# The decoder step's feed-forward: an up projection of seven products instead of eight, a down projection of its own, and the sample tokens' indexer on TensorE

## The chip, the cores and the metric

The kernel runs on one core of one Trainium2 chip. The metric is the device time of one execution in microseconds (us), the median of several runs.

## The reference, cut to what matters

One layer of a decoder handles 2048 prompt tokens and 8 sample tokens. All arrays are float32, with D = 1024 and D_FF = 2816.

```python
z = rmsnorm(x) @ w_in                       # one input projection, columns split between the mixers
# A: an indexer scores all earlier keys, the best 256 of each query are attended (8 heads of 64)
score = sum_h w[t,h] * relu(q_idx[t,h] . k_idx[s]) ;  idx = top_k(score, 256)
# B: pooling over trailing windows;  C: attention to 256 memory tokens
x = x + concat(A, B, C) @ w_out
u = rmsnorm(x) @ w_up                       # 1024 -> 2 * 2816, [g, v]
g, v = conv3(u)                             # causal, per channel
x = x + (silu(g) * v) @ w_down              # 2816 -> 1024
```

For the sample tokens the indexer scores 8192 cached keys of each token, which lie in pages: `dots[key, h] = relu(q_idx[h] . k_idx[key])`, weighted and summed over 8 heads.

## The kernel before, in words

Products of float32 are made on TensorE (PE) from two float32r parts, high and low, as three passes: high x high, high x low, low x high. A helper, `split_psum` (L224 ScalarE, L225 VectorE), makes the two parts of a tile: ScalarE (ACT) writes the high part, VectorE (DVE) subtracts it and writes the low one.

The stages follow one another: a first projection with the indexer's scores of the 16 blocks of 128 prompt tokens (0 to about 330 us; matmuls `pj` are the projection, `isc` the scores, which ACT evicts as `rl`); a second projection and the choice of keys (to about 640); attention by four groups of heads over 16 blocks (to 1184; the probabilities are transposed in `apt`, summed with the values in `ax`, and a block's result leaves as `ao` to the DRAM scratch `mix_d`); the output projection (to 1374), which adds the residual and makes the second norm `h`; the feed-forward (to the end).

The feed-forward goes by three chunks of tokens (768, 776 and 504 + 8 sample tokens), and in each over f = 0 to 21 tiles of 128 hidden channels. For each f, two weight tiles `wr` of 512 KB (gate and value) are loaded and split to `uh`, `ul`; 8 k-steps times three passes (L1675 to L1677) go into PSUM `upg` and `upv`; the convolution reads PSUM (ACT L1679, DVE L1680 and L1682); then silu, the product on GpSimd (POOL, L1692) and a split to `ah`, `al`. Every second f the down products `py` (L1717 to L1719) of all blocks are made and DVE adds them to `yacc` in SBUF (L1720).

The sample tokens' mixers are traced behind the output projection. The scheduler puts their instructions, which have a lower priority, into the feed-forward. Their indexer multiplies on POOL (`ipr`, L1244) and sums on DVE (`dots`, L1246).

All ordinary DMAs are issued by the queue of SyncE (SP), in order: one that waits for its data holds those behind it. Indirect DMAs are issued by POOL. The scheduler fixes each engine's order at build time.

Of the kernel before, what the change touches and what calls it, by code (L numbers as in the profile page):

```python
# [9 lines left out]
F32 = mybir.dt.float32  # L10
# [10 lines left out]
EPS = 1e-6  # L21
# [23 lines left out]
PA, PL = 0, 600  # L45
# [5 lines left out]
# the blocks of each group of heads after which a part of the attention to the memory is traced  # L51
# [25 lines left out]
def bias_onehot():  # L77
    """One-hot bucket of T5 distance x - 127 (none below 0)."""
# [9 lines left out]
def tile_decoder(ctx, tc, I, O, C):  # L88
# [27 lines left out]
    # the sum of two halves of 64  # L116
# [3 lines left out]
    # per-partition signs and masks of the stack (hi, lo, hi, lo) x 32  # L120
# [8 lines left out]
    with tc.tile_pool(name="vps", bufs=1, side="right", space=PSUM) as vps, tc.tile_pool(name="vsb", bufs=1) as vsb:  # L129
        # what the first weights wait for comes first  # L130
# [49 lines left out]
    h_d = dram.tile([KC, 128, S + NS], F32, name="h_d")  # L180
    snew_d = dram.tile([NS, 1], F32, name="snew_d")
# [9 lines left out]
    def rsqrt(ss, p, n, scale):  # L191
        """1 / sqrt(ss * scale + EPS) on [p, n]"""
# [13 lines left out]
    def rsqrt_g(ss, p, n, scale):  # L206
        """the same on GpSimd"""
# [14 lines left out]
    def split_psum(ps, hi, lo):  # L222
        """hi (float32r) and lo (float32r) of a float32 tile"""
# [7 lines left out]
    def split_g(raw, hi, lo, g):  # L231
        """the same, with GpSimd for ScalarE"""
# [7 lines left out]
    def parts_of(b, xh, xl):  # L240
        """what project takes"""
# [4 lines left out]
    def load_x_T(b, xpool, xps, sq):  # L246
        """Block b's tokens, channel-major, in two float32r parts; b = NB: the sample tokens."""
# [17 lines left out]
        # for the second projection  # L265
# [7 lines left out]
    def project(p, xh, xl, outs, spare=None):  # L273
        """outs: (psum, hi weights, lo weights) of [KC] chunks"""
# [25 lines left out]
    # the queries' gains, with the scale of the logits, along the free dimension  # L300
# [1471 lines left out]
```

## Time and profile before

| | |
|---|---|
| runs | 2963.34, 2968.76, 2970.40 us; median 2968.76 |
| profiled execution, its span | 2975.3 us |
| PE busy | 2787.9 us, 94% |
| DVE, ACT, POOL busy | 2241.5, 1365.5, 1187.9 us |
| first and last feed-forward matmul | 1373.8 and 2960.7 us |

The span is the profiled execution's own time; it is 6.5 us above the median of the runs. A busy PE in the profile counts overlapping matmuls once; the pace of matmuls is read from the distance between their starts, since the duration of one covers its pipeline too.

### The profile page before, as it was taken

The numbers are of one execution on the slowest core, as the hardware profiler recorded it, in microseconds if no ns is written. First come the engines' busy times: TensorE is split into PE (matmuls) and PEld (weight loads), VectorE is DVE, ScalarE is ACT, GpSimd is POOL, SyncE is SP. The second block draws the span as 40 slices with busy tenths as digits, with TensorE's granted clock in tenths as the row PEclk, the third lists the DMA queues.
The fourth block names the chain that finished last, engine by engine and source line by source line (L and its number), as shares of the span: only waits on it lengthen the run. The fifth ranks groups of instructions, "written<-read, shape, count | busy, mean of one in ns | idle before, by whom it ended". The sixth has DMA issues, their size and how long they took to land.

```text
span 2975.3 us, 41646 instructions
## 1 busy us (share of the span) xinstructions
PE 2787.9 (94%) x14707; PEld 2428.2 (82%) x14707; DVE 2241.5 (75%) x4459; ACT 1365.5 (46%) x2307; POOL 1187.9 (40%) x1097
## 2 busy tenths in 40 slices
PE   8988788869999999999999999999989999999997
PEld 7877456658988988888988888989878889878886
DVE  5788987967888888446899989898787665666554
ACT  5667686457777777345222222232223333233332
POOL 2333434835745564002888998310436100000000
PEclk9999899879999999999999999999999999999999
DMA  5321334372213223653222222233343322243331
GB/s 183 124 91 54 124 101 123 102 215 80 82 55 99 62 83 99 190 149 115 71 74 75 86 64 73 69 122 121 96 129 92 109 80 82 82 153 106 93 92 53
DMA packets 310311, 301.68 MB, mean 101 GB/s; under 512 B 27444, under 2 KB 272245, under 8 KB 309317
## 3 DMA queue, kind: packets, MB, share of 16 engines
q1 hardware_dynamic: 305236, 285.28, 31.2%
q0 software_dynamic: 4864, 13.73, 1.6%
q8 instruction: 116, 1.90, 0.3%
q14 instruction: 95, 0.77, 0.1%
HBM read 236.36 MB, written 62.89 MB: 101 GB/s over the span
## 4 chain that ended last, share of the span: by engine, by line
PE 58%; DVE 12%; POOL 6%; DMA 3%; issue 2%; ACT 1%; SPq 0%; DVEq 0%; ACTq 0%; POOLq 0%
POOL ipr L1244 4%; PE py L1717 4%; PE upv L1677 4%; PE upv L1675 4%; PE py L1719 4%; PE upv L1676 4%; PE py L1718 4%; PE upg L1677 4%; PE upg L1675 4%; PE upg L1676 4%; PE apt L1055 3%; PE as L1038 2%; DVE dots L1246 2%; PE ax L1058 2%; PE ax L1059 2%
## 5 line engine op out<-in xcount | busy, mean ns | idle before, releaser
L1244 POOL TENSOR_TENSOR ipr<-G,qbc 128x512 f32<-128x512 f32 x256 | 371.1, 1479 | 66.4 <-DVE dots L1246 55.4
L1032 POOL TENSOR_TENSOR t<-R,first 128x128 f32<-128x128 f32 (+15 forms) x128 | 289.0, 2290 | 209.4 <-PE apt L1055 178.9
L1692 POOL TENSOR_TENSOR ct<-ct,ct 128x768 f32<-128x768 f32 (+2 forms) x65 | 118.6, 1824 | 623.8 <-DVE ct L1686 305.6
L1720 DVE TENSOR_TENSOR yacc<-yacc,py 128x512 f32<-128x512 f32 (+1 forms) x408 | 273.1, 680 | 117.8 <-PE py L1719 95.6
L1717 PE MATMUL py<-dh,ah 128*128 128x512 f32 (+1 forms) x704 | 279.8, 399 | 16.0 <-DVE yacc L1720 10.7
L1719 PE MATMUL py<-dh,al 128*128 128x512 f32 (+1 forms) x704 | 275.3, 397 | 3.9 <-DVE al L1697 3.9
L1718 PE MATMUL py<-dl,ah 128*128 128x512 f32 (+1 forms) x704 | 278.1, 395 | 0.0
L224 ACT ACTIVATE uh<-wr 128x1024 fp32r<-128x1024 f32 x132 | 139.6, 1058 | 292.9 <-PE upv L1676 97.3
L1676 PE MATMUL upg<-fhl,uh 128*128 128x390 f32 (+3 forms) x748 | 258.0, 345 | 5.0 <-issue 3.0
L225 DVE TENSOR_TENSOR ul<-wr,uh 128x1024 fp32r<-128x1024 f32 x132 | 176.7, 1339 | 110.4 <-ACT uh L224 110.2
L1676 PE MATMUL upv<-fhl,uh 128*128 128x390 f32 (+3 forms) x748 | 256.9, 343 | 0.0
L1675 PE MATMUL upg<-fhh,uh 128*128 128x390 f32 (+2 forms) x704 | 241.0, 342 | 5.2 <-DVE ct L1682 3.5
L1675 PE MATMUL upv<-fhh,uh 128*128 128x390 f32 (+2 forms) x704 | 240.1, 341 | 3.5 <-ACT ct L1679 2.0
L1677 PE MATMUL upg<-fhh,ul 128*128 128x390 f32 (+2 forms) x704 | 240.7, 342 | 2.8 <-issue 2.8
L1677 PE MATMUL upv<-fhh,ul 128*128 128x390 f32 (+2 forms) x704 | 239.4, 340 | 0.0
L225 DVE TENSOR_TENSOR pl<-apt,ph 128x512 fp32r<-128x512 f32 (+1 forms) x320 | 204.2, 658 | 24.2 <-ACT ph L224 21.9
L1040 DVE CUSTOM_DVE_ANT_0 t<-as,t 128x512 f32<-128x512 f32 (+11 forms) x320 | 189.8, 606 | 41.9 <-PE as L1039 36.7
L224 ACT ACTIVATE ph<-apt 128x512 fp32r<-128x512 f32 (+1 forms) x320 | 173.1, 581 | 62.0 <-PE apt L1055 32.5
L1246 DVE TENSOR_REDUCE dots<-ipr 128x16 f32<-128x512 f32 x256 | 171.8, 679 | 27.5 <-POOL ipr L1244 27.2
L1717 PEld LDWEIGHTS py<-dh,ah 128*128 128x128 f32 (+1 forms) x704 | 132.7, 189 | 44.5 <-DVE yacc L1720 16.5
L1055 PE MATMUL apt<-ident,t 128*128 128x128 f32 x1088 | 164.9, 274 | 3.4 <-DVE pl L225 1.9
L353 ACT ACTIVATE rl<-isc 128x768 f32<-128x768 f32 (+9 forms) x176 | 138.0, 822 | 59.7 <-PE isc L350 42.9
(578 smaller groups left out, 7676.1 us busy)
## 6 DMA issues: line engine op xcount, KB each, us to landing
wr<-in_w_up_dram SPq DMA_DIRECT2D x132, 512.0 KB
dr<-in_w_down_dram SPq DMA_DIRECT2D x66, 512.0 KB
xt<-in_x_prompt_dram SPq DMA_DIRECT2D x16, 512.0 KB
xh_d<-xh SPq DMA_DIRECT2D x16, 512.0 KB
xl_d<-xl SPq DMA_DIRECT2D x16, 512.0 KB
xh<-xh_d SPq DMA_DIRECT2D x16, 512.0 KB
xl<-xl_d SPq DMA_DIRECT2D x16, 512.0 KB
qa<-qh_d SPq DMA_DIRECT2D x64, 128.0 KB
```

What stands on the lines that cost most here:

```text
L224: nc.scalar.activation(hi, ps, AF.Copy)
L225: nc.vector.tensor_tensor(lo, ps, hi.bitcast(F32), op=OP.subtract)
L1032: nc.gpsimd.tensor_tensor(t[:, :N], backward(R[j][:, :N]), nsel[b], op=OP.add)
L1055: nc.tensor.transpose(pt[:, c, j * 128:j * 128 + 128], pn[j][:, (k + c) * 128:(k + c) * 128 + 128], ident)
L1244: nc.gpsimd.tensor_tensor(pr, G[:, u * 512:u * 512 + 512].rearrange("p (k d) -> p k d", d=32), qbc[:, c, None, 32 * h:32 * h + 32].to_broa ...
L1675: nc.tensor.matmul(d, uh[:, k], hh(k, a, e), start=(k == 0), stop=False)
L1676: nc.tensor.matmul(d, uh[:, k], hl(k, a, e), start=False, stop=False)
L1677: nc.tensor.matmul(d, ul[:, k], hh(k, a, e), start=False, stop=(k == KC - 1))
L1717: nc.tensor.matmul(py[:p], ah[:, r0:r0 + p], dh[:, cs], start=(i == 0), stop=False)
L1718: nc.tensor.matmul(py[:p], ah[:, r0:r0 + p], dl[:, cs], start=False, stop=False)
L1719: nc.tensor.matmul(py[:p], al[:, r0:r0 + p], dh[:, cs], start=False, stop=e)
L1720: nc.vector.tensor_tensor(y[:w, cs], y[:w, cs], py[:w], op=OP.add)
```

## The change

**The up projection.** The tokens go by three pairs of halves, of 344, 344 and 340 tokens (`chunks`). With the two halves of the tokens and the two halves of the 1024 channels, and the gate and value tile of an f, the product is one of 2 x 2 blocks, and it is made by seven products instead of eight (Winograd's form of Strassen's scheme). Seven sums of token halves (`b11`, `t1`, `t2`, `b21`, `t3`, `b22`, `t4`, by `operands`) stay in SBUF as two parts each, and seven weight tiles of 512 channels by 128 are loaded and split per f. Three of the seven come from `w_up` as it is, four from weight sums s1 to s4 that lie in DRAM.

**The weight sums.** They are made in DRAM during attention, by 24 steps that `weight_sums` yields, one after every second block of the last three groups of heads. A step issues plain copies from DRAM to DRAM on SP or accumulating DMAs (`accum_op=add`) on POOL, 16 of each in all and 1.44 MB each. An accumulating one is held back by two tiny DMAs on SP (`gates`), one that reads the block's result `ao` and one that reads the sum that it adds to.

**The down projection.** It no longer adds in SBUF. An f's activation is stored to `act_d`; after an up stage `down` reads it back and sums all 22 f in PSUM, for 5, 5 and 6 blocks by two column halves of 512. The order is up, down, operands, down. `x1_d` is added at the end.

**The sample tokens' indexer** (`sample_scores`) runs in the first projection: its 16 units, two per block from block 2 to 9, each gather 128 x 1024 of keys, transpose them by 8 transposes (`tp<-ident,G`), multiply by 8 matmuls of 64 columns (`tp<-qd,gt`), and evict through ACT (two copies, two relu); POOL multiplies by the head weights, DVE sums. The first projection takes the sample tokens first. The other sample mixers stay in the feed-forward, with a lower priority than before (5500 instead of 1500).

**The output projection** stores `x1_d` and `h_d` for all blocks, in the order 4, 5, 2, 3, 0, 1, 6, 7, 14, 15, 12, 13, 10, 11, 8, 9; the first operands are made after eight of them.

```diff
+        for ops in (((s1, v0, 0), (s3, g0, 0)), ((s1, v1, 1), (s3, v0, 1)), ((s2, s1, 0),), ((s2, g0, 1),),
+                    ((s4, s2, 0),), ((s4, g1, 1),)):
+            for k in range(4):
+                def step(after):
+                    for dst, src, add in ops:
+                        if add:
...
+                            dma(o, after[0:1, 0:1])
+                            dma(o, dst[k, 0:1, 0:1])
+                            nc.gpsimd.dma_start(cut(dst, k), cut(src, k), accum_op=OP.add, max_dma_last_dim=5632)
+                        else:
...
+                            dma(dst[k, 0:1, 0:1], after[0:1, 0:1])
+                            dma(cut(dst, k), cut(src, k))
+                yield step
...
                 dma(mix_d[g, :, q0:q0 + TQ], o)
+                step = next(sums, None) if g and b % 2 else None
+                if step:
+                    step(o)
...
+                product(pa, two_parts(g0), "b11", True)
+                nc.scalar.activation(x1, pa[:, :N], AF.Copy, scale=-1.0)
+                product(pc, two_parts(total(1)), "t1", True)
+                nc.scalar.activation(x5, pc[:, :N], AF.Copy)
+                product(pa, two_parts(total(2)), "t2", False)
+                nc.scalar.activation(u2, pa[:, :N], AF.Copy, scale=-1.0)
+                product(pb, two_parts(g1_), "b21", True)
+                nc.vector.tensor_tensor(u[:, 0, lo], pb[:, :N], x1, op=OP.add)
+                product(pa, two_parts(total(3)), "t3", False)
+                nc.vector.tensor_tensor(u[:, 1, hi], pa[:, :N], x5, op=OP.subtract)
+                product(pc, two_parts(total(4)), "b22", False)
+                nc.vector.tensor_tensor(u[:, 0, hi], pc[:, :N], u2, op=OP.add)
...
+                        "t4", False)
+                nc.scalar.activation(u[:, 1, lo], pa[:, :N], AF.Copy)
...
+                for i in range(nb):
+                    b = slice(i * 128, i * 128 + 128)
+                    nc.tensor.matmul(ys[i], ah[:, b], dh, start=s, stop=False)
+                    nc.tensor.matmul(ys[i], ah[:, b], dl, start=False, stop=False)
+                    nc.tensor.matmul(ys[i], al[:, b], dh, start=False, stop=e)
...
-                            nc.vector.tensor_tensor(y[:w, cs], y[:w, cs], py[:w], op=OP.add)
...
-                        nc.gpsimd.tensor_tensor(pr, G[:, u * 512:u * 512 + 512].rearrange("p (k d) -> p k d", d=32),
-                                                qbc[:, c, None, 32 * h:32 * h + 32].to_broadcast([128, 16, 32]), op=OP.mult)
-                        V.tensor_reduce(dots[:, 16 * u:16 * u + 16, h], pr, axis=AX.X, op=OP.add)
...
+                for j in range(8):
+                    nc.tensor.matmul(pd[:, j], gt[j // 4][:, j % 4, :], qd[:, 2 * c:2 * c + 2].rearrange("p b k h -> p (b k h)"),
+                                     start=True, stop=True)
```

What the change moves stands here at three places. First SP's queue where the output projection ends: before, the feed-forward's first weights (`wr<-in_w_up`) stand among the last blocks' loads (`mt`, `ld`).

```order
L1656 DMA wr<-in_w_up_dram 128x8x128 x2
L1138 DMA ld<-in_x_prompt_dram 128x1024
L1133 DMA mt<-mix_d 128x8x128
L1138 DMA ld<-in_x_prompt_dram 128x1024
L1133 DMA mt<-mix_d 128x8x128
L1138 DMA ld<-in_x_prompt_dram 128x1024
L1656 DMA wr<-in_w_up_dram 128x8x128
L1663 DMA dr<-in_w_down_dram 128x1024
L1656 DMA wr<-in_w_up_dram 128x8x128 x2
L1162 DMA x_d<-yacc 128x1024
```

Now the first weights, `wg<-in_w_up`, stand behind the store of the last block's norm, `h_d<-h`.

```order
L1316 DMA h_d<-h 128x8x128
L1305 DMA x_d<-x_17284 128x1024
L1316 DMA h_d<-h 128x8x128
L1799 DMA dr<-in_w_down_dram 128x512 x3
L1316 DMA h_d<-h 128x8x128
L1799 DMA dr<-in_w_down_dram 128x512 x2
L1715 DMA wg<-in_w_up_dram 128x8x128
L1720 DMA wr<-sum_7671 128x4x128
```

The weights moved from ahead of the last blocks' loads to behind the last block's whole norm.

Second SP's queue in attention, in the last group of heads but one or two: before, results (`mix_d<-ao`) and the next queries (`qa`, `qb`, of two parts and two halves).

```order
L1066 DMA mix_d<-ao 128x128
L1007 DMA mix_d<-ao 128x256
L1066 DMA mix_d<-ao 128x128
L958 DMA qa<-qh_d 64x2x256 x2
L958 DMA qb<-ql_d 64x2x256 x2
L958 DMA qa<-qh_d 64x2x256 x2
L958 DMA qb<-ql_d 64x2x256 x2
L1066 DMA mix_d<-ao 128x128 x3
```

Now a step's gate (1x1) and a copy of a piece of a weight sum (`sum_7674<-sum_7672`, s4 from s2) stand between them.

```order
L1188 DMA mix_d<-ao 128x128 x2
L1055 DMA sum_7674<-ao 1x1
L1056 DMA sum_7674<-sum_7672 32x11264
L1128 DMA mix_d<-ao 128x256
L1079 DMA qa<-qh_d 64x2x256 x2
L1079 DMA qb<-ql_d 64x2x256 x2
L1079 DMA qa<-qh_d 64x2x256 x2
L1079 DMA qb<-ql_d 64x2x256 x2
L1188 DMA mix_d<-ao 128x128
```

The queries' loads come behind the gate and the copy.

Third PE in the first projection, where block 3 is scored: before, score matmuls `isc` alternate with the next block's transposes (`tp<-ident,xt`) and projection (`pj`).

```order
L350 MATMUL isc<-ikst,iqst 128x512
L289 MATMUL pj<-wAh,xl 128x404
L263 MATMUL tp<-ident,xt 128x128 x4
L350 MATMUL isc<-ikst,iqst 128x512
L263 MATMUL tp<-ident,xt 128x128 x4
L350 MATMUL isc<-ikst,iqst 128x512
L286 MATMUL pj<-wAh,xh 128x404
L287 MATMUL pj<-wAl,xh 128x404
L286 MATMUL pj<-wAh,xh 128x404
L287 MATMUL pj<-wAl,xh 128x404
L350 MATMUL isc<-ikst,iqst 128x512
```

Now the same scores alternate with the sample tokens' transposes and matmuls, and the next block's projection stands behind all of them.

```order
L348 MATMUL isc<-ikst,iqst 128x512 x2
L427 MATMUL tp<-ident,G 128x128 x4
L348 MATMUL isc<-ikst,iqst 128x512
L427 MATMUL tp<-ident,G 128x128 x4
L348 MATMUL isc<-ikst,iqst 128x512
L434 MATMUL tp<-qd,gt 128x64 x4
L348 MATMUL isc<-ikst,iqst 128x512
L434 MATMUL tp<-qd,gt 128x64 x4
L427 MATMUL tp<-ident,G 128x128 x4
L348 MATMUL isc<-ikst,iqst 128x512 x2
L427 MATMUL tp<-ident,G 128x128 x4
L434 MATMUL tp<-qd,gt 128x64 x4
```

So for blocks 2 to 8 PE meets the projection only after the scores; from block 9 on the order is as before.

## Rows read from the trace of the kernel before

**Rows 1.** The page: its first line and the busy time of the engines
```profile
span 2975.3 us, 41646 instructions
...
PE 2787.9 (94%) x14707; PEld 2428.2 (82%) x14707; DVE 2241.5 (75%) x4459; ACT 1365.5 (46%) x2307; POOL 1187.9 (40%) x1097
```

**Rows 2.** The table of windows: busy us and count by engine, clock, DMA share, GB/s
```profile
core 0: us, PE busy (x) PEld busy (x) DVE busy (x) ACT busy (x) POOL busy (x), PEclk, DMA share, GB/s
0.00:330.00 330.00, 285.68 (x1454) 243.47 (x1455) 257.23 (x556) 221.19 (x379) 122.26 (x157) 0.94 0.35 119
...
640.00:1184.00 544.00, 508.38 (x3699) 469.51 (x3699) 443.49 (x1330) 411.56 (x890) 299.07 (x138) 0.96 0.29 87
...
1474.00:1874.00 400.00, 380.61 (x1947) 348.07 (x1946) 366.47 (x444) 102.72 (x118) 348.29 (x238) 1.00 0.25 75
2180.00:2570.00 390.00, 390.00 (x2008) 349.88 (x2007) 264.11 (x409) 120.77 (x139) 94.58 (x106) 1.00 0.32 95
```

**Rows 3.** Groups by shape, PE, 1373 us to the end
```profile
L1677 PE MATMUL upg<-fhh,ul 128*128 128x390 f32 x352 | 121.5, 345 | 2.8 <-issue 2.8
...
L1675 PE MATMUL upg<-fxh,uh 128*128 128x512 f32 x176 | 69.6, 395 | 0.0
...
L1675 PE MATMUL upg<-fhh,uh 128*128 128x386 f32 x176 | 60.1, 342 | 3.5 <-DVE ct L1682 3.5
```

**Rows 4.** Timeline of PE at 2000 us (start us, us, instruction)
```profile
2000.06 0.34 PE L1677 MATMUL upg<-fhh,ul 128*128 128x390 f32 x1
...
2002.21 0.34 PE L1677 MATMUL upg<-fhh,ul 128*128 128x390 f32 x1
2002.39 0.40 PE L1717 MATMUL py<-dh,ah 128*128 128x512 f32 x1
...
2002.85 0.39 PE L1719 MATMUL py<-dh,al 128*128 128x512 f32 x1
```

**Rows 5.** Timeline of PE at 855 us
```profile
854.66 0.28 PE L1058 MATMUL ax<-ph,vst 128*128 128x256 f32 x1
...
855.01 0.28 PE L1059 MATMUL ax<-pl,vst 128*128 128x256 f32 x1
```

**Rows 6.** The page's costliest groups: count | busy us, mean ns | idle before
```profile
L1244 POOL TENSOR_TENSOR ipr<-G,qbc 128x512 f32<-128x512 f32 x256 | 371.1, 1479 | 66.4 <-DVE dots L1246 55.4
...
L1720 DVE TENSOR_TENSOR yacc<-yacc,py 128x512 f32<-128x512 f32 (+1 forms) x408 | 273.1, 680 | 117.8 <-PE py L1719 95.6
...
L225 DVE TENSOR_TENSOR pl<-apt,ph 128x512 fp32r<-128x512 f32 (+1 forms) x320 | 204.2, 658 | 24.2 <-ACT ph L224 21.9
...
L224 ACT ACTIVATE ph<-apt 128x512 fp32r<-128x512 f32 (+1 forms) x320 | 173.1, 581 | 62.0 <-PE apt L1055 32.5
L1246 DVE TENSOR_REDUCE dots<-ipr 128x16 f32<-128x512 f32 x256 | 171.8, 679 | 27.5 <-POOL ipr L1244 27.2
```

**Rows 7.** Groups of lines, VectorE and then ScalarE, 1373 us to the end
```profile
L1682 DVE SCALAR_TENSOR_TENSOR ct<-upv,convc,ct 128x768 f32<-128x768 f32 (+2 forms) x66 | 60.9, 922 | 0.5
...
L1679 ACT ACTIVATE ct<-upv,convc 128x768 f32<-128x768 f32 (+2 forms) x66 | 59.9, 907 | 8.3 <-PE upv L1677 8.3
```

**Rows 8.** The chain in order of time, from 917 and from 1470 us
```profile
917.09 7.18 DMA mix_d<-ao
...
1469.99 3.67 DMA dr<-in_w_down_dram
```

**Rows 9.** The table of windows, the first 50 us
```profile
0.00:50.00 50.00, 41.54 (x214) 37.44 (x215) 26.94 (x152) 25.68 (x48) 10.39 (x24) 1.00 0.71 231
```

**Rows 10.** Timeline at the end of the output projection, VectorE, then ScalarE
```profile
1373.99 1.22 DVE L1152 TENSOR_TENSOR yacc<-opy,ld 128x1024 f32<-128x1024 f32 x1
...
1375.31 1.06 ACT L1088 ACTIVATE hn<-yacc 128x1024 f32<-128x1024 f32 x1 [0.83 <-DVE yacc L1152]
...
1380.49 1.15 ACT L1090 ACTIVATE hn<-yacc,rsy 128x1024 f32<-128x1024 f32 x1 [0.29 <-DVE rsy L203]
...
1387.19 1.14 ACT L1172 ACTIVATE hn<-oph,vcol 128x128 f32<-128x128 f32 x4 [3.76 <-PE oph L1095]
```

More of the change, by code (lines that the diff above doesn't have):

```diff
@@ L326, in tile_decoder @@
     junkD = tp_.tile([128, S], mybir.dt.uint8, name="junkD")
-    scp = pool("scp", side="right", stack=scst)
-    for b in range(11, LATE):
-        sc[b] = scp.tile([128, (b + 1) * TQ], F32, name=f"sc{b}")
     dst_ = ExitStack()
@@ L420, in load @@
             return p, xh, xl
-        ahead = load(0)
+        ahead = load(NB)
         wAh = ap_.tile([128, KC, NA], F32R, name="wAh")
@@ L458, in tile_decoder @@
                 dma(v_s.rearrange("l b t h d -> (l b t) (h d)"), z[:p, 552:808])
-                break
+                units = sample_scores(z, pool("six", bufs=2, side="right", stack=sst), ap2, aps)
+                next(units)
+                continue
             q0 = b * TQ
@@ L519, in tile_decoder @@
                 late[b] = iqst, iws
+            if b < 10:
+                for _ in range(2):
+                    with later(SA):
+                        next(units)
+        mapped()
     scl = pool("scl", side="right", stack=scst)
@@ L1015, in tile_decoder @@
             mem_attend(*next(units))
+        sums = weight_sums()
         for g in range(4):
@@ L1127, in tile_decoder @@
             split_psum(raw, woh[k], wol[k])
-        n0 = bounds[1] // TQ
-        for i, b in enumerate(list(range(n0, NB - 1)) + list(range(n0)) + [NB - 1]):
+        order = [4, 5, 2, 3, 0, 1, 6, 7, 14, 15, 12, 13, 10, 11, 8, 9]
+        for i, b in enumerate(order):
             q0 = b * TQ
@@ L1178, in tile_decoder @@
[L1178 to L1187 removed]
+            dma(x1_d[q0:q0 + TQ], x1)
@@ new lines, in tile_decoder, with put @@
+            h = ox.tile([128, KC, 128], F32, name="h", bufs=2)
+            def put(half, ph):
+                for i in range(4):
+                    k = half * 4 + i
+                    if half:
+                        nc.scalar.activation(h[:, k], ph[:, i], AF.Copy, scale=g2(k))
+                    else:
+                        nc.vector.tensor_scalar(h[:, k], ph[:, i], g2(k), None, op0=OP.mult)
+            second_norm(x1, TQ, hn, ops, put)
+            dma(h_d[:, :, q0:q0 + TQ].rearrange("k p t -> p k t"), h)
@@ new lines, in tile_decoder @@
+        stage = lambda: fu.tile([128, 2, 2 * NH + 2], F32, name="u").rearrange("p j t -> p (j t)")
+        for ci in range(2):
+            up(ci)
+            down(640 * ci, 5, 0, 0)
+            operands(ci + 1, stage)
+            down(640 * ci, 5, 0, 1)
+        up(2)
+        fpx = pool("fpx", bufs=2, side="right", stack=st, space=PSUM)
+        for q0, q1, w in ((0, 4, 512), (4, 5, 128)):
+            pt = bank(fpx)
+            for q in range(q0, q1):
+                src = ups[:, 2 * q - 2:2 * q, :] if q else hal.rearrange("p t j f -> p (t j f)")
+                nc.tensor.transpose(pt[:4 * NF, 128 * (q - q0):128 * (q - q0) + 128], src, ident)
+            o = fc_.tile([128, 2 * NH], F32, name="ct")
+            nc.scalar.activation(o[:4 * NF, :w], pt[:4 * NF, :w], AF.Copy)
+            for q in range(q0, q1):
+                r = o[:4 * NF, 128 * (q - q0):128 * (q - q0) + 128]
+                if q == 0:
+                    dma(conv_p[0, 0].rearrange("j (f c) -> (j f) c", c=128), r)
+                    continue
+                for e in range(2):
+                    dma(conv_s[0, 2 * q - 2 + e, 1].rearrange("(f c) -> f c", c=128), r[2 * NF * e:2 * NF * e + 2 * NF])
@@ L1744 @@
+        fr = pool("fr", bufs=2, side="right", stack=st)
+        for c in range(2):
+            down(1280, 6, NS, c, fpx, fr)
 _INS = ["x_prompt", "x_sample", "mem_prompt", "cache_k", "cache_v", "cache_idx_k", "cache_mem_k", "cache_mem_v",
```

482 lines of the change are left out of this document (253 added, 229 removed).

## The prediction

> **What bounds the kernel now.** I read the page's head first, then the windows by stage, then groups by shape in the feed-forward and the starts of single matmuls. PE is busy 94% of the span [rows 1], and a share over stages hides where it is not. By windows [rows 2] it is 286 of 330 us in the first projection, 508 of 544 in attention, 381 of 400 in the feed-forward while the sample tokens' indexer runs there, and 390 of 390 in the feed-forward after that. So in the feed-forward, over half of the span, PE's own pace is the limit: what is taken off its matmuls there is taken off the time, as long as the other engines keep up. The idle of the indexer's window lies beside POOL at 348 of 400 us and DVE at 366: there the two other engines are late.
>
> **The up projection, the main term.** From starts, 12 steps of 390 columns take 2.15 us, 0.179 each, and two of 512 columns 0.46, 0.230 each [rows 4]; three of 256 columns 0.35, 0.117 each [rows 5]. Between the last two ends a line gives 386 columns 0.177, 384 columns 0.176, 344 columns 0.158, 340 columns 0.156. Counts before [rows 3]: 390 columns in six groups of 352 (two PSUM tiles, three passes), 2112; 512 columns 1056; 386 and 384 columns 1056 each. That is 378.5 + 242.9 + 186.9 + 185.9, 994 us. After: 22 f x 7 products x 4 k x 3 passes = 1848 per pair of halves, 1848 x (0.158 + 0.158 + 0.156) = 872 us. Saved: **122 us** (115 to 125, for reading starts to 0.01 us). The down products keep their number and width: nothing.
>
> **The indexer leaves the feed-forward.** With it go 371 us of POOL and 172 of DVE [rows 6]; both were cover or brake for PE, worth the 19.4 us that PE idles in its window [rows 2]. **−19** (−25 to −8: some of the idle there is the down weights' arrival, as the 3.67 us of `dr` [rows 8]). The 273 us of `yacc` adds on DVE [rows 6] go too; with PE at 390 of 390 beside them they are worth nothing by themselves.
>
> **Whether DVE and ACT keep up in the up stage.** One f takes PE 13.2 us (872 / 66). DVE has seven low parts of 512 at 658 ns [rows 6], 4.6 us; four convolution steps of 688 at 922 x 688 / 768 [rows 7], 3.3; three sums from PSUM of 344, each between 440 (658 by its columns) and 658 ns, about 1.5: 9.4 us, 71%. ACT has seven high parts at 581 ns, four evictions of about 0.45, two of 688 at 0.81 [rows 6, 7] and a silu and copies of the same size: about 8.3 us, 63%. Both fit on average. But three products accumulate on one that must first be evicted, seven tiles of weights are split just ahead of use, and only the interleaving of two f's hides it. Without that cover the four evictions between products of one f would stand bare, each about 0.45 us plus a hand-off as long: 3.6 us per f, 240 in all. With it, nothing. I take 0.3 us per f, **+20** (0 to 60), nearer to hidden because the order puts a second f's matmuls between.
> Weights per f are 512 KB and five times 256 KB, with the stored activation 2.2 MB in 13.2 us, 167 GB/s; 231 GB/s at a share of 0.71 [rows 9] puts that at 51% of the DMA engines. It fits too.
>
> **The boundary.** Before, the feed-forward's weights are loaded amid the last blocks and its first matmul follows at once on the output projection's last. After, they stand on SP behind the last block's `h_d<-h`. PE then waits for that block's chain: add 1.22, square 1.06, scale 1.15, four evictions 1.14 [rows 10], eight transposes and the reciprocal root about 2, hand-offs about 1; then 3.7 for a 512 KB load as `dr` [rows 8] and 1.2 for its split. 12.5 us; **+13** (8 to 17). Queued behind `h_d<-h` are all weight loads, and PE is the one who waits.
>
> **Changes between up and down, and the tail.** The first `dr` and `al` loads can run ahead, since `down` has buffers of its own. Two us at each of a few changes, less a shorter tail (before, 14.6 us follow the last matmul): **+5** (0 to 15).
>
> **First projection.** Added on PE are 16 units of 8 transposes and 8 matmuls of 64 columns, each between nothing and the 0.117 of 256 columns [rows 5], about 0.1 in practice: 1.6 us per unit, 26 us. PE has 44 us of idle there, but spread out. ACT gets per unit two copies of 512 at 0.58 [rows 6] and two relu of about 0.4: 31 us. And the scores of blocks 2 to 8 no longer alternate with the next projection, so that PE meets ACT's pace there with only the sample's matmuls as cover. If all fits in idle time, +5; if all the PE work shows and each of 8 blocks loses 3 us more, +50. **+30**, nearer to the upper end because PE is already the busiest engine of the window.
>
> **Attention.** Sixteen copies and sixteen accumulating transfers of 1.44 MB. At the rate of [rows 9] (325 GB/s at a full share) one takes 4.4 us or more of all DMA engines, 32 of them 141 us; what an accumulating one takes no row shows. Attention's DMA share is 0.29 of 544 us, so there is room, yet a query load or a `mix_d` store that meets one comes 4 to 9 us later, and `ao` has one buffer: the chain already has a store of 7.18 us on it [rows 8]. SP also waits at each gate about 2 us, with the next `qa` and `qb` behind. If the loads are far enough ahead, nothing; if each of 24 steps costs 2.5 us, 60. **+22**.
> What speaks against this part stands in the Trainium skill, "DMA: Bandwidth & Descriptors", section "Issuing engines are not separate DMA queues": transfers of every issuing engine run on the same 16 DMA engines and interleave, so POOL's queue is no escape for the accumulating ones. "Collectives: The Full Stack", section on the fold count, adds that a reduce needs two source reads and so ran at about half of a copy's rate. By that, an estimate, an accumulating transfer takes 8.8 us and the 32 take 211 us, and the term would be some 35 instead of 22. No row here shows one.
>
> **Sum.** −122 − 19 + 20 + 13 + 5 + 30 + 22 = −51 against the span of 2975.3: 2924. The profiled execution is 6.5 us above the runs' median, so I forecast **2916** for the median of the changed kernel.
>
> **Rivals.**
> (a) *The weight sums hold up attention, and the kernel is slower.* The steps come every second block over three groups, about 408 us for 24 steps, 17 us apart. The sums chain on one another (s1, then s2, then s4), and SP's gate for a step waits for the accumulation four steps before. If an accumulating transfer takes under 17 us, POOL's queue keeps up and the price is the term above. At 30 us, sixteen take 480 us in 408, and SP stands still with queries and results behind it: +72 or more beyond the sum, and with the interference then doubled about 100: 3016. It decides from about 27 us. For: no accumulating row in the trace, and the price is unknown. Against: 1.44 MB at the rate of [rows 9] is a sixth of that.
> (b) *The up stage is bound by evictions and splits.* If the bare waits come to 1.3 us per f, 86 us instead of 20: 2982, no faster. For: DVE at 71% with dependent chains. Against: PE was at 390 of 390 with DVE at 264 of 390, 68% [rows 2].
> (c) *All of it is hidden.* Coupling 0, attention 0, first projection +10, boundary +8: −122 − 25 + 18 + 3 = −126, 2843. For: room on every engine. Against: the order in the first projection.
> (d) *The saving in matmuls is not there*, because short matmuls cost as much as long ones. The 256-column starts of [rows 5] exclude it but for a few us.
>
> **Chances.** My forecast with terms off by their bounds: 0.6; (c) 0.12; (b) 0.12; (a) 0.13; others on the slow side 0.03. A measurement of this kernel tells about 0.3% (9 us) from no change, so "same" is 2960 to 2978. The forecast's cases lie all but 0.02 below that; (b) is half in it. Faster 0.76, same 0.08, slower 0.16. The range runs from 2855, a few us above all hidden, to 2985, where (b) at its price still lies; (a) stays out. The forecast's own range is 2880 to 2955.
>
> **What would show it.** Right: no `ipr` in the feed-forward; up products at 0.156 to 0.158 between starts, 13.2 to 13.6 us per f; PE idle of some 13 us between the last `opy` and the first `py`; PE at 400 of 400 in later windows; a first projection longer by some 30 us. Wrong: gaps before `py` that end with DVE or ACT on evictions or splits, of over 0.5 us per f (b); rows of the accumulating transfers over 17 us, with SP's `gates` waiting tens of us and PE idle before `as` (a); or loads `wr` that land after their use. The weakest terms are the first projection and attention, for which nothing alike is in the trace.

## The result and the profile after

The changed kernel takes 3055.64 us (median of 4 runs, 3051.4 to 3065.07), the kernel before 2969.36; the ratio is 1.0306, 95% interval 1.0277 to 1.0335. It is slower by 86 us, where I forecast 53 us faster. The profiled execution has a span of 3051.3 us, 76 more than before's.

The page's head of the changed kernel:

```profile
span 3051.3 us, 46352 instructions
...
PE 2747.7 (90%) x15363; PEld 2417.9 (79%) x15363; DVE 2179.2 (71%) x4511; ACT 1676.2 (55%) x3013; POOL 1024.3 (34%) x1097
```

PE is busy 40 us less than before [rows 1], and the span is longer: PE waits more. Where, is read from its windows, cut at the stages: first projection, attention, output projection, what lies between its last matmul and the feed-forward's first, then first up stage, second up stage, third up stage, and the last down stage with the tail.

```profile
0.00:373.00 373.00, 324.90 (x1813) 278.83 (x1814) 260.85 (x576) 245.04 (x438) 147.18 (x194) 0.95 0.39 126
...
692.00:1315.00 623.00, 528.93 (x3699) 479.97 (x3699) 445.15 (x1328) 407.29 (x888) 314.93 (x150) 0.93 0.54 144
1315.00:1524.00 209.00, 193.90 (x883) 160.10 (x882) 100.82 (x263) 77.58 (x136) 18.08 (x10) 0.95 0.61 183
1524.00:1547.00 23.00, 5.11 (x20) 4.14 (x20) 14.32 (x54) 7.87 (x17) 1.14 (x5) 0.56 0.64 186
1547.00:1838.00 291.00, 290.48 (x1825) 290.04 (x1826) 226.97 (x316) 180.34 (x313) 50.53 (x61) 0.99 0.61 178
...
2023.00:2352.00 329.00, 302.31 (x1855) 293.08 (x1854) 288.57 (x518) 184.65 (x323) 191.49 (x169) 0.97 0.66 190
...
2534.00:2817.00 283.00, 282.60 (x1812) 281.67 (x1811) 220.38 (x343) 169.38 (x298) 78.06 (x104) 1.00 0.56 166
2817.00:3051.00 234.00, 213.18 (x913) 163.43 (x912) 86.76 (x151) 62.87 (x92) 9.08 (x47) 0.97 0.47 145
```

The third up stage has PE at 282.6 of 283 us: nothing waits there. The starts of its matmuls of 340 columns, 20 steps apart in 3.12 us, 0.156 each:

```profile
2659.76 0.32 PE L1736 MATMUL py<-b22l,wh 128*128 128x340 f32 x1
...
2662.88 0.32 PE L1736 MATMUL py<-t3l,wh 128*128 128x340 f32 x1
```

So the saving in matmuls is real. It is outweighed elsewhere. The stages by the first and last starts of their matmuls (the tile view), for all runs told below; "gap" is from the output projection's last matmul to the feed-forward's first, "feed-forward" from its first to its last matmul, "time" the median of the runs:

| run | second projection begins | attention | output projection | gap | feed-forward | time |
|---|---|---|---|---|---|---|
| before | 321 | 546 | 190 | 0 | 1586 | 2969 |
| changed | 374 | 623 | 208 | 24 | 1488 | 3056 |
| e1 no sums | 373 | 536 | 199 | 26 | 1503 | 2969 |
| e2 tiny DMAs only | 372 | 540 | 202 | 24 | 1505 | 2976 |
| e5 copies only | 374 | 561 | 202 | 25 | 1499 | 2993 |
| e6 copies by POOL | 372 | 615 | 207 | 25 | 1495 | 3057 |
| e13 quarter pieces | 374 | 613 | 206 | 25 | 1488 | 3041 |
| e3 three `ao` | 375 | 595 | 208 | 24 | 1489 | 3045 |
| e7 sums early | 392 | 545 | 196 | 25 | 1499 | 3043 |
| e4 no units | 337 | 640 | 207 | 24 | 1488 | 3029 |
| e11 units late | 324 | 636 | 206 | 26 | 1596 | 3121 |
| e14 no mixers | 372 | 630 | 208 | 24 | 1424 | 2992 |
| e8 pools | 375 | 627 | 208 | 6 | 1526 | 3079 |
| e15 pools, no mixers | 374 | 626 | 206 | 7 | 1440 | 2987 |
| e10 `hal` by DVE | 371 | 627 | 208 | 24 | 1495 | 3064 |
| e9 sums by POOL | 374 | 533 | 198 | 22 | 1833 | 3302 |
| e12 both of e9, e11 | 326 | 531 | 202 | 27 | 1923 | 3343 |
| e16 sums in the first up stage | 371 | 537 | 201 | 22 | 1763 | 3228 |
| e17 e16 and e8 | 371 | 537 | 202 | 7 | 1767 | 3216 |
| e18 e17 in tiles of `down` | 370 | 531 | 202 | 7 | 1525 | 2977 |

The second projection takes 316 to 319 us in all of them but e3 (340) and e7 (366). Of the 76 us between the two profiled executions, the first projection makes +53, the second +2, attention +77, the output projection +18, the gap +24, and from the feed-forward's first matmul to the end −98 (1601.5 to 1504.0).

In attention the waits of PE name what is late:

```profile
engine line waited for: us in total, times, longest us
PE as L1161 <- DMA qb<-ql_d: 17.8, 6, 7.5
PE ax L1180 <- ACT ao L1187: 14.2, 5, 7.0
...
PE as L1160 <- DMA qa<-qh_d: 6.0, 4, 3.1
...
PE as L1102 <- DMA qb<-mql_d: 4.1, 2, 2.4
...
ACT ao L1187 <- DMA mix_d<-ao: 40.0, 9, 10.0
```

ScalarE's writing of `ao` waits 40 us for the store of the one before. In the trace of before the same three waits were shorter:

```profile
PE ax L1058 <- ACT ao L1065: 6.3, 4, 2.9
PE as L1039 <- DMA qb<-ql_d: 2.8, 3, 1.0
ACT ao L1065 <- DMA mix_d<-ao: 7.0, 4, 3.4
```

The page's list of DMA issues has the accumulating transfers, 11.8 us from issue to landing in the median (10.6 to 21.0). The last two of the 16 start only in the output projection, the last at 1338.7 us. In attention's window the queue that POOL feeds moved 20.19 MB, 14 transfers, and its packets took 17.3% of the 16 engines' 623 us, 7.7 us of all of them per transfer:

```profile
sum<-in_w_up_dram POOLq DMA_DIRECT2D x16, 1408.0 KB, 11.8
...
q0 software_dynamic: 3808, 20.19, 17.3%
```

### The profile page after: what moved, and what is told of

Its sections match the earlier page's. It is cut to its first block, busy times and chain, and to the rows that moved or that the text cites. A ratio compares the mean times of both kernels' runs of the same rounds, so it can differ in the third digit from the quotient of the medians.

```text
span 3051.3 us, 46352 instructions
## 1 busy us (share of the span) xinstructions
PE 2747.7 (90%) x15363; PEld 2417.9 (79%) x15363; DVE 2179.2 (71%) x4511; ACT 1676.2 (55%) x3013; POOL 1024.3 (34%) x1097
## 5 line engine op out<-in xcount | busy, mean ns | idle before, releaser
L225 ACT ACTIVATE wh<-wr 128x512 fp32r<-128x512 f32 x330 | 205.0, 626 | 164.9 <-PE py L1736 137.8
L226 DVE TENSOR_TENSOR wl<-wr,wh 128x512 fp32r<-128x512 f32 x330 | 272.7, 828 | 31.9 <-ACT wh L225 31.8
L1819 PE MATMUL py<-dl,ah 128*128 128x512 f32 x704 | 278.3, 400 | 11.5 <-DVE dl L226 11.5
L1820 PE MATMUL py<-dh,al 128*128 128x512 f32 x704 | 271.9, 396 | 0.0
L1818 PE MATMUL py<-dh,ah 128*128 128x512 f32 x704 | 200.5, 400 | 12.5 <-DVE ct L1833 6.8
L1819 PEld LDWEIGHTS py<-dl,ah 128*128 128x128 f32 x704 | 134.5, 191 | 47.4 <-DVE dl L226 15.2
L1166 ACT ACTIVATE t<-t,amn 128x128 f32<-128x128 f32 (+15 forms) x128 | 153.8, 1203 | 24.5 <-DVE amn L1165 22.6
L1769 DVE SCALAR_TENSOR_TENSOR ct<-u,convc,ct 128x688 f32<-128x688 f32 (+1 forms) x132 | 136.9, 1037 | 40.8 <-ACT ct L1768 36.6
L1180 PE MATMUL ax<-ph,vst 128*128 128x256 f32 x544 | 148.1, 296 | 17.9 <-ACT ao L1187 14.2
L1181 PE MATMUL ax<-pl,vst 128*128 128x256 f32 x544 | 151.4, 303 | 1.7 <-DVE pl L226 1.5
## 6 DMA issues: line engine op xcount, KB each, us to landing
sum<-in_w_up_dram POOLq DMA_DIRECT2D x16, 1408.0 KB, 11.8
```

The lines of the kernel that those rows point to most:

```text
L225: nc.scalar.activation(hi, ps, AF.Copy)
L226: nc.vector.tensor_tensor(lo, ps, hi.bitcast(F32), op=OP.subtract)
L1166: nc.scalar.activation(t[:, :N], t[:, :N], AF.Exp, bias=m, accum_out=sm[:, j:j + 1])
L1180: nc.tensor.matmul(pxf, vst(k + c)[:, g, :], ph[:, c, :], start=(k + c == 0), stop=False)
L1181: nc.tensor.matmul(pxf, vst(k + c)[:, g, :], pl[:, c, :], start=False, stop=(k + c == b))
L1818: nc.tensor.matmul(ys[i], ah[:, b], dh, start=s, stop=False)
```

## The experiments

Single edits against the changed kernel, unless said otherwise.

### The weight sums in attention

**e1, no sums.** `total` reads `w_up[0:512, f]` four times in place of `sum_d`.

```diff
-                step = next(sums, None) if g and b % 2 else None
+                step = None
```

> Leaves out all 24 steps of the weight sums (copies, accumulating transfers, gates); the up stage reads the upper half of the gate tile of w_up in place of each sum, the same bytes in the same pieces. Theory A (the sums' steps lengthen attention): attention, 625 us from its first score matmul to the output projection's first matmul in the changed kernel, falls to 545 to 555, as before the change, and the time by 65 to 80 us to about 2980. Rival B (attention is longer for another part of the change, such as the pools or the order): it stays at 600 or more and the time within 20 us of 3056. The up stages should not change either way.

Measured: attention 536 us, the output projection 199, time 2969.1, ratio to the kernel before 0.9998 (0.9979 to 1.0016). Theory A holds, rival B falls; attention and the time come out some 10 us below A's figures, and the feed-forward is 15 us longer, which was not expected and not followed up. Everything else in the change together neither wins nor loses. Attention's window of e1:

```profile
692.00:1228.00 536.00, 505.00 (x3699) 466.79 (x3699) 442.13 (x1328) 408.39 (x888) 299.18 (x136) 0.97 0.30 85
```

Of the 87 us between this window and the changed kernel's, 63 are idle time of PE and 24 are busy time: the same 3699 matmuls keep PE busy for 528.9 us instead of 505.0, at a mean granted clock of 0.93 of full speed instead of 0.97. So part of the price comes as slower matmuls in a stage where PE stops more often.

How far attention differs by itself is seen in kernels that have the same attention: 531 to 537 us in the six without sums (e1, e9, e12, e16, e17, e18), 623 to 631 in the changed kernel, e8, e10, e14 and e15 (636 and 640 in e11 and e4). A difference of 8 us or less in a single trace shows little.

**e2, tiny DMAs only; e5, copies only.**

```diff
-                            nc.gpsimd.dma_start(cut(dst, k), cut(src, k), accum_op=OP.add, max_dma_last_dim=5632)
...
-                            dma(cut(dst, k), cut(src, k))     # e2 alone
```

> Keeps every tiny gating DMA at its place, leaves out the 16 copies and the 16 accumulating transfers; the up stage reads as in the run without sums. If the traffic of 1.44 MB pieces is what delays the query loads and the result stores (theory A1): attention 550 to 565 us, time about 2985. If SP standing at the gates, with the loads behind it, is what costs (theory A2): attention 600 to 625, time 3035 to 3056.

> Keeps the gates and the 16 plain copies from DRAM to DRAM on SP's queue, leaves out the 16 accumulating transfers; the up stage reads tiles of w_up in place of the sums. The run with the tiny DMAs alone had attention at 540 us, the changed kernel 623. If the accumulating transfers carry the cost (two sources, 11.8 us to landing): attention 545 to 565, time 2980 to 2995. If the plain copies carry it, since queries and results stand behind them in the same queue: 600 to 623, time 3030 to 3050. If both by their bytes: 575 to 590.

Attention's windows of e2 and of e5:

```profile
691.00:1231.00 540.00, 506.01 (x3700) 465.42 (x3700) 442.20 (x1329) 408.08 (x888) 298.80 (x136) 0.97 0.30 85
```

```profile
689.00:1250.00 561.00, 513.39 (x3700) 468.90 (x3700) 444.74 (x1331) 408.96 (x889) 298.96 (x136) 0.96 0.41 124
```

The gates cost 4 us over e1, no more than that spread, the 16 copies 21 more (1.3 each), the 16 accumulating transfers 62 more (3.9 each). The DMA share goes from 0.30 to 0.41 and, with all, 0.54: far from full, and PE still waits. From these shares and windows the copies took 68 us of all DMA engines, 4.2 each, where an accumulating one took 7.7. A2 falls as e2 tests it; e2's attention lies below both of its cases. e5 is in its first case with attention and time: the accumulating ones carry three quarters. What e2 can't test is the gates beside the traffic. There SP's waits at them are 34 us, against 9 in e2:

```profile
SPq L1051 <- DMA gates<-ao: 19.3, 8, 6.4
...
SPq L1056 <- DMA sum<-ao: 15.1, 11, 7.3
```

How much of the 62 us goes by way of these waits stays open, as no run has the accumulating transfers without gates.

**e6, copies by POOL; e13, quarter pieces; e3, three buffers for ao.**

```diff
-                            dma(cut(dst, k), cut(src, k))
+                            nc.gpsimd.dma_start(cut(dst, k), cut(src, k))        # e6
...
-        cut = lambda a, k: a[k].rearrange("p (c n) -> p c n", c=2)
+        cut = lambda a, k, j: a[k][32 * j:32 * j + 32].rearrange("p (c n) -> p c n", c=2)    # e13
...
-                o = wq.tile([128, 256], F32, name="ao")[:, 0:128]
+                o = wq.tile([128, 256], F32, name="ao", bufs=3)[:, 0:128]        # e3
```

> The changed kernel whole, but the 16 plain copies are issued by POOL instead of SP. If what costs is that loads of queries and stores of results stand behind a copy of 1.44 MB in one queue: attention falls from 623 to 575 to 600, time 3025 to 3040. If the transfers share the DMA engines whichever engine issues them, as the section on issuing engines of the page DMA: Bandwidth & Descriptors in the Trainium skill says: attention 610 to 635, time within 15 us of 3056.

> The changed kernel whole, but each of the 24 steps is cut in four of a quarter of the bytes (0.36 MB), 96 in all, three after every two blocks of all four groups of heads instead of one after every second block of three. If queries and results come late because they meet a burst of 1.44 MB: attention falls from 623 us to 560 to 585, time 3010 to 3035. If the delay goes with the bytes moved (or with the number of steps): attention 615 to 650, time 3050 to 3085.

> The changed kernel whole, but the buffer of a block's result ao is threefold, so that ScalarE need not wait for the store of the one before. If the late store is a cause by itself (ScalarE waits 40 us for it in the profile of the changed kernel): attention 585 to 605 instead of 625, time 3020 to 3040. If the query loads are late in any case and the wait only moves there: 615 to 625, time 3045 to 3056.

e6: 615 us and the time of the changed kernel, within its rival's bounds. That agrees with the Trainium skill, "DMA: Bandwidth & Descriptors", section "Issuing engines are not separate DMA queues": another issuing engine is no other path. e13: 613 us, in neither of its cases; it also spreads the steps over all four groups of heads. So bursts are at most a small part (10 us); PE's waits only change name, `qa` 26.3 us and `qb` 14.1 in its trace. e3: attention 595, but it begins later, and from the second projection's first matmul to the output projection's first it is 934.9 against 941.4 us: 6.5 us, no more than the spread. So neither the queue, the piece nor the one buffer makes the price; it goes with the transfers, and not by their bytes alone, as an accumulating one of the same 1.44 MB cost three times a copy.

**e7, sums early.** The 24 steps stand in blocks 4 to 15 of the first projection and 2 to 13 of the second.

```diff
+            if b >= 4:
+                next(sums)(z)
...
+            step = next(sums, None) if b >= 2 else None
+            if step:
+                step(zf)
```

> The changed kernel whole, but the 24 steps of the weight sums are spread over blocks 4 to 15 of the first projection and 2 to 13 of the second instead of attention. Attention falls to 535 to 550. If the projections have room (their loads of 0.5 MB are ahead, and PE waits there for other engines): they lengthen by under 15 us together, time 2965 to 2990. If their block loads are held up as the queries were: 30 to 80 us more, time 3000 to 3050.

Attention 545, but the first projection is 19 us and the second 47 us longer: of 78 us won, 66 are given back. In both places tried the transfers are paid. Waits in the second projection of e7, PE first, then DVE and ACT, which wait for stores before they write the next `ql` and `mqh`; in the changed kernel's second projection the first two were 5.2 and 8.1 us and the last two do not occur:

```profile
PE tp L953 <- DVE ql L957: 20.8, 5, 8.8
...
PE apt L1055 <- DMA kr<-out_dram: 13.0, 3, 11.7
...
DVE ql L957 <- DMA ql_d<-ql: 17.8, 3, 9.8
...
ACT mqh L965 <- DMA mqh_d<-mqh: 13.5, 2, 8.2
```

### The first projection

**e4, no units; e11, units late.** e4 drops the loop over the units; e11 leaves the sample tokens last and makes the units among the sample mixers.

```diff
-                    with later(SA):
-                        next(units)        # e4
...
-        for b in [NB] + list(range(NB)):
+        for b in range(NB + 1):            # e11
```

> Leaves out the 16 sample score units in the first projection (gathers, transposes, matmuls, evictions; the scores are a ramp in their place), keeps the sample tokens first. The second projection begins 52.7 us later than before the change. If the units and the order that they force cost most of it: it begins at 333 to 342 us instead of 373.7, and the time falls by 32 to 40. If the sample tokens' projection ahead of the others (all weights must have landed for it) costs most: 350 to 365 us, and the time falls by 10 to 20.

> The changed kernel whole, but the sample tokens stay last in the first projection and the 16 score units run on TensorE among the other sample mixers in the feed-forward. The second projection should begin at 320 to 324 us instead of 373.7, if the early place and nothing else made the 52.7 us. The feed-forward takes 26 us of matmuls and transposes more, 1510 to 1540. Time 3025 to 3055; if the units' chain of evictions holds the up products in PE's order, the feed-forward is over 1550 and nothing is won.

e4: the second projection begins at 336.8 us; the units and their order cost 37, and the start is still 16 later than before the change. With neither (e11) it is 324, so the sample tokens ahead cost 13 of the 16. The time of e4 falls only by 27, since attention is 640 there. e11 is in its second case: the feed-forward takes 1596 us, 107 more than the changed kernel, for 26 us of matmuls; why so much was not followed up.

### The feed-forward

**e14, no mixers.** The sample mixers' section is replaced by zeros in `h_d` and `scb`.

> Leaves out the sample tokens' mixers in the feed-forward (their choice of keys, attention, pooling, output projection and convolution state; zeros in their place), all else as changed. In the changed kernel the feed-forward from its first to its last matmul takes 1488 us, where its own matmuls at their pace make 872 + 510 us. If the sample mixers among its instructions cost the rest: 1385 to 1410 us, time 2960 to 2980. If evictions, splits and the changes between up and down cost it: 1440 to 1470 us, time 3005 to 3040.

Feed-forward 1424 us, 64 less, and time 2992: between its two cases, so both hold in part. Its three up stages:

```profile
1553.00:1844.00 291.00, 290.10 (x1821) 289.17 (x1822) 223.36 (x306) 179.87 (x313) 49.23 (x61) 0.99 0.61 177
2019.00:2300.00 281.00, 280.93 (x1785) 280.65 (x1784) 215.93 (x296) 171.70 (x296) 60.70 (x61) 1.00 0.60 175
2476.00:2758.00 282.00, 281.97 (x1811) 281.56 (x1810) 219.99 (x343) 169.19 (x298) 78.04 (x104) 1.00 0.55 166
```

PE is busy throughout. The windows hold 1785 to 1821 of a stage's 1848 up matmuls in 281 to 291 us (the others stand among the down products), 0.156 to 0.160 each, where the sum had 872 / 3 = 291 for all. So evictions and splits cost nothing. The other 42 us over 872 + 510 lie in the down stages and the changes between them, 12 to 16 us in each first half of columns and about 10 in the last stage.

**e8, pools; e15, pools without mixers; e10, hal by DVE.**

```diff
-        fw = pool("fw", bufs=4, stack=st)
-        fq = pool("fq", bufs=8, stack=st)
+        fc_ = pool("fc", bufs=3, stack=st)
+        fu = pool("fu", bufs=2, stack=st)
         fx = pool("fx", stack=st)
...
-        fu = pool("fu", bufs=2, stack=st)
-        fc_ = pool("fc", bufs=3, stack=st)
+        fw = pool("fw", bufs=4, stack=st)
+        fq = pool("fq", bufs=8, stack=st)
...
-                nc.gpsimd.tensor_copy(hal_of(f), u[:, :, n:n + 2])
+                nc.vector.tensor_copy(hal_of(f), u[:, :, n:n + 2])    # e10
```

> The changed kernel whole, but the feed-forward's pools are laid out in another order, so that the first weight tiles no longer lie where the last norms h were, and their loads stand on SP ahead of the last two stores of h. If the place of these loads makes the gap at the boundary: it falls from 24 us to 4 to 10, time 3035 to 3041. If the last norms themselves hold PE (the transposes stand ahead of the first product in its order): 17 to 24 us, time 3049 to 3056.

> As the run without the sample mixers, and with the feed-forward's pools in the order that lets the first weights come ahead of the last norms. In the run with that order alone the gap at the boundary fell from 24 to 6 us, but the feed-forward grew from 1488 to 1526. If the order of the pools only moved the sample mixers to a worse place: gap 5 to 8 us and a feed-forward as in the run without the mixers, time 15 to 20 us below it. If the order itself makes the up stage wait: the feed-forward is 25 to 40 us longer than without it.

> The changed kernel whole, but the small copies of the last two columns of u (hal) are made by VectorE instead of POOL, where they stand behind the sample tokens' indirect gathers (in the changed kernel's profile one such wait holds PE for 9.7 us). If that queue is a main part of the 81 us that the feed-forward loses to its floor: feed-forward 1455 to 1475 instead of 1488. If the sample mixers' other work on VectorE and ScalarE is: 1480 to 1490, time within 10 us of 3056.

The gap falls to 6 and 7 us, so the place of the first loads made it. In e15 the first up stage is 11 us longer (302 instead of 291) and the down stage behind it about 6: most of the gap is given back, and the time is 5 us below e14, not 15 to 20; why that stage is longer stays open. In e8 the third up stage has 306 of 337 us and the time is worse; that stage is undisturbed without the mixers, so there it is their place. e10 (3064) shows that the queue of gathers on POOL, which the longest wait in the changed kernel's second up stage hangs on, is no main cause.

### The sums without DRAM arithmetic

**e9, sums by POOL; e12, with the units late; e16, in the first up stage alone; e17, with the pools; e18, in idle tiles.** The core of e16 (e9 does it in all three stages, without the store):

```diff
+        seq = [0, 1, NB] + list(range(2, NB))
...
+        for i, b in enumerate(seq):
...
+                    ws = [fs.tile([128, 4, 128], F32, name=f"ws{i}") for i in range(4)]
+                    for t, x, y in ((0, v0, v1), (1, ws[0], g0), (2, g0, v0), (3, ws[1], g1_)):
+                        nc.gpsimd.tensor_tensor(ws[t], x, y, op=OP.add)
+                        dma(sum_d[t][:, :, f * 128:f * 128 + 128].rearrange("k p n -> p k n"), ws[t])
```

e18 takes `ws` from tiles `dr` and `al` of `fd`.

> The changed kernel whole, but no sums in DRAM: the up stage loads the gate and the value tile of an f (two loads of 512 KB instead of one of 512 and five of 256 KB) and POOL adds the four sums of 128 x 512 in SBUF, again for each pair of halves. If the weight sums' transfers are the cause and POOL has room (four adds at about 1.5 us and the product of 2.0 per f of 13.2 us): attention 530 to 545 us, feed-forward 1485 to 1520, time 2955 to 2990. If POOL with the sample tokens' gathers becomes late in the up stage, or slows VectorE: feed-forward over 1540, time over 3010.

> Both: sums by POOL in the up stage and the score units late. If the two causes add: about the time of the run with sums by POOL less 10 to 30 us, 2930 to 2975, at or below the kernel before. If POOL, now with gathers, adds and head weights at once, is late: over 2985.

> The changed kernel whole, with two edits. The four sums of an f are added by POOL in SBUF in the first up stage alone and stored to DRAM from there, and the second and third up stage load them as before; nothing of the sums is left in attention. And the sample tokens come third in the first projection instead of first. If the two causes found are right and of their sizes: attention 530 to 545 us instead of 623, the output projection 195 to 202 instead of 208, the second projection begins at 358 to 364 us instead of 373.7, and the first up stage is 10 to 40 us longer than 291 because VectorE slows beside POOL; time 2960 to 2995. If the stores and POOL hold up the first up stage by more than that: over 3010.

> As the run before, and with the feed-forward's pools in the order that lets the first weights come ahead of the last norms. If the gap at the boundary is won here: 5 to 15 us less than the run before, 2950 to 2985, and the first kernel with the seven products that may equal the kernel before. If the pools move the sample mixers to a worse place again: 10 to 30 us more.

> As the run before, but the sums of the first up stage lie in tiles of the down stage (dr, al), which are idle then, so that the feed-forward needs no more memory than the changed kernel. By the listing of PE's order, in the two runs before all 117 matmuls of the sample mixers stand in one piece between the first up and the first down stage; here they are spread as in the changed kernel. If the memory did that: the 317 us without down matmuls between the first up and the first down stage go, attention 537 us, the gap at the boundary 7, the first up stage about 330, feed-forward 1515 to 1550, time 2960 to 3000, between 50 and 95 us below the changed kernel. If the mixers stay slow because POOL and VectorE are late: over 3050.

e9, e12, e16 and e17 had attention at 531 to 537 us, as in e1, and lost 275 us and more in the feed-forward. e16's windows of the first up stage and of what follows it, and its longest waits of PE behind that:

```profile
1448.00:1779.00 331.00, 306.35 (x1857) 300.95 (x1856) 313.41 (x347) 178.29 (x315) 189.63 (x150) 0.96 0.59 174
1779.00:2096.00 317.00, 57.32 (x142) 23.75 (x142) 171.58 (x415) 38.29 (x63) 109.06 (x126) 0.51 0.26 73
```

```profile
PE sa L1524 <- DVE L L1491: 91.2, 1, 91.2
PE sb L1376 <- DVE scn L1374: 71.8, 10, 10.1
PE sb L1552 <- ACT svh L225: 44.2, 16, 4.0
```

For 317 us PE has the sample mixers almost alone (`sa`, `sb`), waiting for DVE most of the time. Of the 152 instructions of PE that write `sa` or `sb` in this trace, 132 stand there, between the last matmul of the first up stage and the first down product; in the changed kernel 145 of 151 stand behind the first down product. The sums' own pool `fs` takes 8 KB of memory per partition; e18, which needs none, has the mixers spread again (134 of 151 behind the first down product) and a feed-forward of 1525 us. e17, which differs from e18 in this pool alone, has the block. So the pool made it; by which of its dependences was not traced. e18's windows, attention, first up stage, third up stage:

```profile
687.00:1218.00 531.00, 501.51 (x3700) 462.57 (x3699) 442.61 (x1331) 409.16 (x889) 299.00 (x136) 0.98 0.30 87
...
1427.00:1766.00 339.00, 307.84 (x1849) 301.02 (x1848) 322.15 (x399) 180.88 (x322) 187.86 (x149) 0.96 0.58 172
...
2452.00:2735.00 283.00, 282.76 (x1815) 282.03 (x1814) 220.11 (x343) 169.19 (x298) 78.36 (x105) 1.00 0.56 166
```

e18 leaves nothing out and takes 2977.12 us, 79 below the changed kernel and 1.0040 (1.0025 to 1.0055) of the kernel before: it does not beat it. Its second projection begins at 370 us: the sample tokens in third place won 3 us or 4, not 13.

## Why the prediction was wrong, point by point

- **The up projection, −122: right.** 0.156 per matmul as forecast, and PE's pace in all three stages without the mixers (e14).
- **DVE and ACT in the up stage, +20: too much.** Without the mixers the stages stand at PE's pace (e14). Rival (b) falls.
- **The indexer leaves, −19, and changes and tail, +5 (0 to 15): not as forecast.** With +20 the three add up to +6, and the sum had −116 for the feed-forward; it was −98, so they came to +24. Before, the feed-forward was 82 us over the pace of its matmuls (1586 against 994 + 510), after, 106: 64 are the mixers that remain and 42 the down stages and their changes (e14), and the tail behind the last matmul is no shorter (15 and 16 us). What the mixers cost before was not run, so how much of the −19 was won stays open.
- **Attention, +22 (0 to 60): the step that failed.** It was 77 (87 against e1), beyond the upper bound, and 9 more in the output projection (208 against 199 in e1), for which the sum had nothing. The mechanism was the one told, late query loads and result stores, but its size was bounded by "each of 24 steps costs 2.5 us"; a step cost 3.6, the copies 1.3 and the accumulating transfers 3.9 each. I took room in the DMA share (0.29) for cover, priced an accumulating transfer as a copy (4.4 us of all DMA engines; the copy's 4.2 bears that out, the other took 7.7), and had nothing for the lower granted clock. Rival (a) had the right place and sign at another price: it set 27 us per transfer as the point of decision, and at 11.8 us, where it allowed no more than the term, the kernel was already slower. SP did not stand still as it had it: its longest wait at a gate was 7.3 us.
- **First projection, +30 (5 to 50): 53.** The units and their order were 37; the missed part is the sample tokens ahead, 13 of the other 16, where I priced nothing: their projection takes both halves of the weights at once, and before, the first block's ran while these arrived. That this is why the first place costs them is argued, not shown: in third place (e16) the sample tokens won back only 3.
- **Boundary, +13 (8 to 17): 24.** I took the last norm's chain alone. The norms lag two blocks behind the matmuls (their scratch `hn` has one buffer; that this holds them back is argued), so two norms of 7.6 us stand in a row, and two loads of `dr` stand between `h_d<-h` and `wg`. SP's queue after the last-but-two block's norm:

```profile
1523.84 0.37 SPq L1316 DMA_DIRECT2D h_d<-h  x1
...
1531.44 0.37 SPq L1316 DMA_DIRECT2D h_d<-h  x1
1531.91 2.21 SPq L1799 DMA_DIRECT2D dr<-in_w_down_dram  x3
1539.04 0.38 SPq L1316 DMA_DIRECT2D h_d<-h  x1
1540.72 1.18 SPq L1799 DMA_DIRECT2D dr<-in_w_down_dram  x2
1541.99 0.38 SPq L1715 DMA_DIRECT2D wg<-in_w_up_dram  x1
```

The output projection's last matmul is at 1523.2 us; the last store is issued at 1539.0, the first weights at 1542.0. With these loads ahead of the last norms the gap was 6 us (e8).

- **The output projection, 0 in the sum: 18.** 9 are the sums (e1), two of whose accumulating transfers run there and not in attention; the rest goes with PE waiting 10.4 us for `hn` there.
- **The sum.** 2924 less 6.5 is 2918, not 2916; the 2 us change nothing above.

The Trainium skill's rule on the reduce, in "Collectives: The Full Stack", section on the fold count, raised the term to 35 and was the better pointer, though it is told there for rings of cores. The traces come near its half rate: an accumulating transfer took 7.7 us of all DMA engines, a copy 4.2. PE lost three times as much per accumulating transfer as per copy.

## What to carry to other kernels

A mean share of the DMA engines far below one (here 0.54) did not mean room for bulk transfers beside a stage that waits for small loads and stores: price them by what PE loses per transfer, in a run that has them alone. Of a scheme that saves a share of PE's work, count first what prepares its operands; here the sums alone took 87 us of the 122 that the eighth product had cost, and the longer first projection (53) and the gap (24), which came with the rest of the change, took more than what was left. A pool of 8 KB added to a late stage moved small matmuls of another section into one block: look at the order again after each edit.

## What was not expected of the hardware

VectorE's subtraction `wl` of 128 x 512, with both operands in SBUF, took 684 ns (from `wg`) and 877 ns (from `wr`) in the changed kernel's third up stage, where GpSimd is busy for 78 of 283 us. In e9's first up stage, with GpSimd adding (busy for 175 of 300 us), it took 981 ns from `wg` and 1027 ns from the sums `ws`. The first row is the changed kernel's, the others are e9's:

```profile
L226 DVE TENSOR_TENSOR wl<-wg,wh 128x512 fp32r<-128x512 f32 x41 | 28.1, 684 | 9.9 <-ACT wh L225 9.9
...
L226 DVE TENSOR_TENSOR wl<-wg,wh 128x512 fp32r<-128x512 f32 x39 | 38.3, 981 | 0.5 <-ACT wh L225 0.5
L226 DVE TENSOR_TENSOR wl<-ws,wh 128x512 fp32r<-128x512 f32 x78 | 79.9, 1027 | 8.9 <-ACT wh L225 8.9
```

So GpSimd's idle time was not free to use: in e18 VectorE is busy for 322 of the first up stage's 339 us, where the changed kernel's takes 291. That the two engines hold each other up is argued from these means; no run has the same work of VectorE with GpSimd at rest.
